# A weight block split earlier in the mask stage, one block moved ahead of it and one behind it: a hybrid decoder block on one Trainium2 core

## The chip, the core and the metric

The kernel runs on one core of one Trainium2 chip. A core has a matrix engine (TensorE, PE in the rows; PEld is its weight load), a vector engine (VectorE, DVE), a scalar engine (ScalarE, ACT), GpSimd (POOL) and SyncE (SP), which here issues nearly all DMAs. Each engine works through its own queue in order; semaphores tie the queues together. The metric is the device time of one execution in microseconds (us). TensorE's clock has two levels, 1.2 and 2.4 GHz; the profile gives the granted clock as a share of the higher one.

## The reference

```python
def reference(x, p, ...):                       # x: (1, 512, 1024) float32
    xn = _rmsnorm(h, ln_mix_g[i]); z = xn @ w_in[i]
    ...                                          # S5 scan, spatial gating, output projection
    h = h + mix @ w_out[i]
    hn = _rmsnorm(h, ln_ffn_g[i])
    h = h + _peer(hn, peer_wq[i], peer_keys[i], peer_u[i], peer_v[i])
    gate = jax.nn.sigmoid(_rmsnorm(h, ple_norm_g[i]) @ ple_w_gate[i])
    h = h + gate * (p[i] @ ple_w_proj[i])
    return _rmsnorm(h, final_g)

def _peer(xn, wq, keys, u_tab, v_tab):           # 16384 experts = 128 x 128 product keys
    q = (xt @ wq).reshape(t, 8, 2, 128)
    sc = einsum('thkd,hknd->thkn', q, keys)
    ...                                          # top 16 of each half, top 16 of the sums
    gates = softmax(top_s)
    act = gelu(einsum('td,thkd->thk', xb, u_tab[experts])) * gates
    return einsum('thk,thkd->td', act, v_tab[experts])
```

The change lies in `_peer`.

## The kernel before

The experts are not gathered for most tokens. For 384 of the 512 tokens the kernel multiplies all 16384 rows of `u_tab` and of `v_tab` and masks the result; the first 128 tokens (`NS`) gather their experts by indirect DMA. The 128 x 128 experts make 128 blocks (`NK`) of 128 experts. A **u block** is one such block of `u_tab` times the normalised tokens: `b_mm` issues 24 matmuls (8 slices of the depth, three products of float32r high and low parts, by `mm3`), and ScalarE's gelu leaves the result in a slot of `gab`, or, for the blocks in the list `FAR`, in a tile `far` that a DMA writes to DRAM (`fard`) and a later one reads back. A u block's weights go through three steps: `b_load` (SP fetches `ust`, three buffers), `b_split` (ScalarE casts `ust` to the high part `uh`, then another engine subtracts to give the low part `ul`, two buffers each), `b_mm`. `b_step(n)` does `b_load(n + 3)`, `b_split(n + 1)`, `b_mm(n)`. `b_split` gives the subtraction to GpSimd in four pieces, except for u blocks numbered from `PREM` to `NPRE`, where VectorE does it in one. `UORD` is the order in which u blocks are taken.

The part of `tile_hybrid_block` around the change runs in this order, and the order is written out by hand:

- **Retrieval**: scores, top-16 lists, and u blocks 0 to 33 between them (`ahead(upto)` takes u blocks until number `upto` - 1). Then `softmax_b` on VectorE, and `slots`, which transposes indices and gates on TensorE and turns them into `keyn` and `gpart`.
- **Mask stage**: `one_hots(0)`, `ahead(PRE + PREX + PREY)`, which is u block 34, and 96 steps of 4 tokens. For each pair of steps VectorE makes one `onehot` tile (`one_hots`, two instructions, `OB` = 2 buffers); for each step TensorE multiplies 12 small bf16 matmuls out of it into `pgm`, and ScalarE copies `pgm` to `stg`. Steps 2k and 2k + 1 read one-hot tile k, and tile k + 1 is put into the queue ahead of step 2k. Every eight steps a DMA writes `stg` to `gd` in DRAM. After every fourth step stands a `b_step`: u blocks 35 to 58, 24 of them.
- **Main loop**: for each of the 128 blocks `r`, the masks `gread` come back from `gd`, `a_gate` multiplies them into the block's `gab` slot, `a_split` and `v_split` make `ah`, `al`, `vh`, `vl`, and `y_mm(r)` multiplies 24 matmuls of 512 columns (`yp`). The remaining u blocks 59 to 127 are taken here. Before `r` = 0 stand `a_gate(0)`, `a_split(0)`, `v_split(0)`, `a_gate(1)`; `r` = 0 takes u block 59 ahead of `y_mm(0)`. The tiles `vh`, `vl` lie in memory that the retrieval and mask stages' tiles have used, `far` among them, so that their first writer waits for the last DMA out of that memory.

The lines that set the counts before:

```python
PRE = 33; PREX = 1; PREY = 1; NPRE = AHEAD + SPILL   # 59
PREM = PRE + PREX + PREY                             # 35
o = gw.tile([P, 4, TG // 2, NK, 2], BF16, name="onehot", bufs=OB)    # OB = 2
ahead(PRE + PREX + PREY + (n + 1) * (NPRE - PRE - PREX - PREY) // len(steps))
```

Of the kernel before, what the change touches and what calls it, by code (L numbers as in the profile page):

```python
# [29 lines left out]
H = 8  # L30
# [10 lines left out]
AHEAD = 40  # L41
# [26 lines left out]
PRE = 33  # L68
SPILL = 19
GPIECE = 256  # L70
FLEAD = 24
PREX = 1
PREY = 1


# [2 lines left out]
NPRE = AHEAD + SPILL  # L78
PREM = PRE + PREX + PREY
UORD = []  # L80
for _i in range(AHEAD):
    UORD.append(_i)
    if _i >= PRE0 - SPILL // 2 and len(UORD) - _i - 1 < SPILL and _i % 2 == 0:
        UORD.append(FAR[len(UORD) - _i - 1])
UORD += FAR[len(UORD) - AHEAD:]
UORD += [_b for _b in range(NK) if _b not in UORD]
assert sorted(UORD) == list(range(NK)) and set(UORD[:NPRE]) == set(range(AHEAD)) | set(FAR)

# [16 lines left out]
def tile_hybrid_block(ctx: ExitStack, tc: tile.TileContext, x, p_t, cols_d, rows_d, w_in, s5_b, s5_c, glu_w, ws_t,  # L105
# [35 lines left out]
    def pst(name, pool=None):  # L141
        return (pool or ps).tile([P, 512], F32, name=name, tag="ps")
# [13 lines left out]
    def split_sb(hi, lo, src, eng=None, piece=GPIECE):  # L156


        S.copy(hi, src)  # L159
        if eng is not G:  # L160
            V.tensor_tensor(lo, src, hi.bitcast(F32), op=ALU.subtract)  # L161
            return
        h, l, s = (a if len(a.shape) == 2 else a.rearrange("p a b -> p (a b)") for a in (hi.bitcast(F32), lo, src))
        for o in range(0, l.shape[1], piece):
            sl = slice(o, o + piece)
            G.tensor_tensor(l[:, sl], s[:, sl], h[:, sl], op=ALU.subtract)  # L166
# [692 lines left out]
    def b_load(n):  # L859
        if n < NB:  # L860
            BS[n] = ub.tile([P, ND, P], F32, name="ust", bufs=3)
            nc.sync.dma_start(BS[n], wq[n] if n < 2 * H else ut[UORD[n - 2 * H]])

    def b_split(n, eng=G):
        if n < NB:
            hi = ub.tile([P, ND, P], F32R, name="uh")
            lo = ub.tile([P, ND, P], F32R, name="ul")
            if PREM <= n - 2 * H < NPRE + 1:
                split_sb(hi, lo, BS[n], V)
            else:  # L870
                split_sb(hi, lo, BS[n], eng, GPIECE if n < 2 * H + NPRE else D)
            BS[n] = hi, lo

    def b_mm(n):
        if n >= NB:
            return
        hi, lo = BS.pop(n)
        p_ = pst("pq", ps2)
        t0 = 0 if n < 2 * H else NS
        for c in range(ND):  # L880
            mm3(p_[:, 0:T - t0], (hi[:, c, :], lo[:, c, :]), (hn[c][0][:, t0:T], hn[c][1][:, t0:T]), c == 0, c == ND - 1)
        if n < 2 * H:
            QT[n] = qw.tile([P, T], F32, name="qt")
            S.copy(QT[n], p_)
        else:
            n = UORD[n - 2 * H]
            if n in FAR:
                t = fr.tile([P, TD], F32, name="far")
                S.activation(t, p_[:, 0:TD], AF.Gelu)
                nc.sync.dma_start(fard[FAR.index(n)], t)  # L890
            else:
                ga[n] = slot(n)
                S.activation(ga[n], p_[:, 0:TD], AF.Gelu)  # L893
# [5 lines left out]
    def far_load(n):  # L899
        ga[n] = slot(n)  # L900
        nc.sync.dma_start(ga[n], fard[FAR.index(n)])

    def b_step(n):
        b_load(n + 3)
        b_split(n + 1)
        b_mm(n)

    keys = qw.tile([P, 2 * H, NK], F32, name="keys", bufs=1)
# [115 lines left out]
    done = 1  # L1024

    def ahead(upto):
        nonlocal done
        while done < upto:
            b_step(2 * H + done)
            done += 1  # L1030
# [5 lines left out]
    for i in order:  # L1036
        S.activation(gates[i], gates[i], AF.Exp)
    ahead(PRE + PREX)
    for i in order:
# [27 lines left out]
    def v_load(r):  # L1067
        st = vg.tile([P, D], F32, name="vst")
        nc.sync.dma_start(st, uv[r * P:(r + 1) * P, D:])
        VS[r] = st  # L1070

    def g_load(r, n=NDC):
        if r % RG == 0:
            gr = vg.tile([P, NDC, RG, TC], F32, name="gread")
            nc.sync.dma_start(gr[:, 0:n].rearrange("p c r t -> p c (r t)"), gd[:, r // RG, 0:n, :])
            GR[r // RG] = gr
# [4 lines left out]
    steps = [(i, c, t0) for i in range(NS // P, NT) for c in range(P // TC) for t0 in range(0, TC, 4)]  # L1081
    OH = {}

    def one_hots(n):

        i, c, t0 = steps[n * TG // 4]
        keyn, gpart = trs[i]
        g = (c * TC + t0) // TG
        o = gw.tile([P, 4, TG // 2, NK, 2], BF16, name="onehot", bufs=OB)
        flat = lambda a: a.rearrange("p z t r e -> p (z t) r e")  # L1090
        two, three = [P, TG, NK, 2], [P, 3 * TG // 2, NK, 2]
        pairs = lambda a: a[:, g].rearrange("p z (t e) -> p (z t) e", e=2)[:, :, None, :]
        V.tensor_tensor(o[:, 2:4], keyno[:, None].to_broadcast([P, 2, TG // 2, NK, 2]), pairs(keyn).to_broadcast(two),
                        op=ALU.is_equal)
        V.tensor_tensor(flat(o[:, 0:3]), o[:, 2:3].to_broadcast([P, 3, TG // 2, NK, 2]), pairs(gpart).to_broadcast(three),
                        op=ALU.mult)
        OH[n] = o

    one_hots(0)
    ahead(PRE + PREX + PREY)  # L1100
    for n, (i, c, t0) in enumerate(steps):
        gn, ga0 = n * 4 // TG, n * 4 % TG
        if ga0 == 0 and (gn + 1) * TG < 4 * len(steps):
            one_hots(gn + 1)
        if n == len(steps) - VPRE:
            v_load(0)
            v_load(1)
        if t0 == 0:
            stg = gw.tile([P, NK, TC], F32, name="stg")
        pg = pst("pgm")  # L1110
        o = OH[gn]
        for a in range(4):
            for z in range(3):
                t, e = divmod(ga0 + a, 2)
                PE.matmul(pg[:, a * P:(a + 1) * P], o[:, 3, t, :, e], o[:, z, t, :, e], start=z == 0, stop=z == 2)
        S.copy(stg[:, :, t0:t0 + 4].rearrange("p r t -> p t r"), pg.rearrange("p (t r) -> p t r", t=4))
        if n == len(steps) - 1:
            V.tensor_copy(GR[0][:, NDC - 1], stg[:, 0:RG, :])
        if t0 + 4 == TC:
            nc.sync.dma_start(gd[:, :, (i * P - NS) // TC + c, :], stg.rearrange("p (a r) t -> p a (r t)", r=RG))  # L1120
            if n == len(steps) - 1 - TC // 4:
                g_load(0, NDC - 1)
        ahead(PRE + PREX + PREY + (n + 1) * (NPRE - PRE - PREX - PREY) // len(steps))
    gs.close()
    ret.close()

# [12 lines left out]
    def v_split(r):  # L1139
        st = VS[r]  # L1140
        vh = vb.tile([P, D], F32R, name="vh")
        vl = vb.tile([P, D], F32R, name="vl")
        split_sb(vh, vl, st, V)
        VS[r] = vh, vl

    def a_gate(r):
        if r < NK:
            a3 = ga[r].rearrange("p (c t) -> p c t", c=NDC)
            V.tensor_tensor(a3, a3, GR[r // RG][:, :, r % RG, :], op=ALU.mult)  # L1149
# [110 lines left out]
    a_split(0)  # L1260
    v_split(0)
    a_gate(1)
    for r in range(NK):
        if r + 2 < NK:
            v_load(r + 2)
        if r + 4 < NK:
            g_load(r + 4)
        if r + FLEAD in FAR:
            far_load(r + FLEAD)
        s0 = nb  # L1270
        while nb < ns[r]:
            n = 2 * H + nb
            b_load(n + 3)
            if n + 3 >= NB:
                wg_load(n + 3 - NB)
            b_split(n + 1)
            nb += 1
        while kg < min(NK, ks[r] + 2):
            gather(kg)
            kg += 1  # L1280
        k0 = kd
        while kd < ks[r]:
            dot_step(kd)
            kd += 1
        for n in range(s0, nb):
            assert UORD[n] - NAHEAD < r
            b_mm(2 * H + n)
        if r + 1 < NK:
            a_gate(r + 2)
            a_split(r + 1)  # L1290
            v_split(r + 1)
        if kd > k0:
            act_step(k0, kd - k0)
        for k in range(k0, kd):
            y_step(k)
        j = r - (NK - SEND)
        if 1 <= j:
            wg_load(j + 2)
        if 0 <= j <= 4:
            wg_split(j, WGE[j])  # L1300
        elif j == 5:
            wg_split(5, "V")
            wg_split(6, "V")
        if j == 0:
            assert kd == NK
            V.tensor_tensor(hsb[:, 0, :], hsb[:, 0, :], y0, op=ALU.add)
            row_tile(None, "fin", hrow0)
        if j == TR:
            t_rows(0, 0, ps2)
            t_rows(0, 1, ps2)  # L1310
        if j == TR + 1:
            t_norm(0)
        if r == NK - SEND - 4:
            assert nb - NK + NAHEAD >= 0 and r + 1 >= NK - NAHEAD + -(-NT * D // TD)
            hsb = gab[:, 0:NT * D].rearrange("p (i d) -> p i d", i=NT)
            for i in range(NT):
                nc.sync.dma_start(hsb[:, i, :], hd[i])
        y_mm(r)
# [91 lines left out]
```

## Time and profile before

| | us |
|---|---|
| median of 3 runs (1580.32 to 1581.36) | 1580.43 |
| the profiled execution's own time | 1581.07 |
| its span in the trace | 1579.4 |
| mask stage, from the first one-hot (485.73) to the last mask step's end (680.03) | 194.3 |
| main loop, from the first matmul of `y_mm(0)` (693.1) to those of the last `y_mm` (1524.1) | 831 |

The profile lists busy time per engine, and per line and tile. A row of the timeline gives start and duration of an instruction, then engine, line, operation, output and inputs, and in brackets how long the engine had been idle before it and what ended that. Instructions overlap a little at their ends, so the time that one takes from its engine is read from one start to the next.

### The profile page before, as it was taken

The numbers are of one execution on the slowest core, as the hardware profiler recorded it, in microseconds if no ns is written. First come the engines' busy times: TensorE is split into PE (matmuls) and PEld (weight loads), VectorE is DVE, ScalarE is ACT, GpSimd is POOL, SyncE is SP. The second block draws the span as 40 slices with busy tenths as digits, with TensorE's granted clock in tenths as the row PEclk, the third lists the DMA queues.
The fourth block names the chain that finished last, engine by engine and source line by source line (L and its number), as shares of the span: only waits on it lengthen the run. The fifth ranks groups of instructions, "written<-read, shape, count | busy, mean of one in ns | idle before, by whom it ended". The sixth has DMA issues, their size and how long they took to land.

```text
span 1579.4 us, 22413 instructions
## 1 busy us (share of the span) xinstructions
PE 1506.2 (95%) x8195; PEld 1305.6 (83%) x8195; DVE 1354.7 (86%) x2512; ACT 661.9 (42%) x1121; POOL 603.3 (38%) x478
## 2 busy tenths in 40 slices
PE   8799989999997888889999999999999999999998
PEld 5456778899997888878888888888888888888886
DVE  9897645899998888859898999999899999989774
ACT  3655433333335666643333333333333333333354
POOL 2001214477880000015455555545455455555201
PEclk9999999999999999999999999999999999999999
DMA  6132033224343566788899998899899989999841
GB/s 254 41 100 68 27 117 123 81 94 139 136 142 116 179 222 194 236 276 310 309 331 343 336 336 321 327 336 341 316 350 337 344 317 346 331 329 330 301 165 67
DMA packets 129711, 369.90 MB, mean 234 GB/s; under 512 B 9024, under 2 KB 63040, under 8 KB 113088
## 3 DMA queue, kind: packets, MB, share of 16 engines
q1 hardware_dynamic: 111168, 234.24, 42.7%
q0 software_dynamic: 18432, 134.23, 22.9%
q8 instruction: 64, 1.05, 0.3%
q14 instruction: 47, 0.39, 0.1%
HBM read 333.24 MB, written 35.19 MB: 233 GB/s over the span
## 4 chain that ended last, share of the span: by engine, by line
PE 33%; issue 7%; DVE 6%; POOL 5%; DMA 5%; ACT 0%; POOLq 0%; DVEq 0%; ACTq 0%
PE yp L153 7%; PE yp L154 7%; PE yp L152 6%; DMA g<-in_uv,idx 5%; PE pq L154 3%; PE pq L152 3%; PE pq L153 3%; POOL ul L166 3%; POOL g L1135 2%; DVE vl L161 2%; DVE gab L1149 1%; DVE act L1171 1%; DVE g L1167 1%; PE pg L152 1%; PE pg L154 1%
## 5 line engine op out<-in xcount | busy, mean ns | idle before, releaser
L166 POOL TENSOR_TENSOR ul<-ust,uh 128x256 fp32r<-128x256 f32 (+1 forms) x268 | 359.6, 1367 | 369.5 <-ACT uh L159 369.3
L152 PE MATMUL pq<-hnh,uh 128*128 128x384 f32 (+1 forms) x1152 | 397.2, 345 | 0.8 <-DVE hnl L170 0.8
L154 PE MATMUL pq<-hnh,ul 128*128 128x384 f32 (+1 forms) x1152 | 394.7, 343 | 1.7 <-POOL ul L166 1.7
L153 PE MATMUL pq<-hnl,uh 128*128 128x384 f32 (+1 forms) x1152 | 393.4, 342 | 0.0
L1135 POOL DMA_INDIRECT g<-in_uv,idx x128 | 209.1, 1634 | 313.6 <-DVE y L1178 298.1
L153 PE MATMUL yp<-vl,ah 128*128 128x512 f32 x768 | 303.4, 395 | 10.1 <-DVE vl L161 10.0
L152 PE MATMUL yp<-vh,ah 128*128 128x512 f32 x768 | 300.8, 392 | 4.4 <-ACT vh L159 4.4
L154 PE MATMUL yp<-vh,al 128*128 128x512 f32 x768 | 302.0, 393 | 0.0
L893 ACT ACTIVATE gab<-pq 128x384 f32<-128x384 f32 x109 | 53.7, 492 | 429.5 <-PE pq L154 429.5
L154 PEld LDWEIGHTS pq<-hnh,ul 128*128 128x128 f32 x1152 | 216.6, 188 | 8.6 <-POOL ul L166 3.1
L152 PEld LDWEIGHTS pq<-hnh,uh 128*128 128x128 f32 x1152 | 216.9, 188 | 8.2 <-DVE hnl L170 1.0
L153 PEld LDWEIGHTS pq<-hnl,uh 128*128 128x128 f32 x1152 | 216.9, 188 | 7.4 <-DVE hnl L170 0.2
L161 DVE TENSOR_TENSOR vl<-vst,vh 128x1024 fp32r<-128x1024 f32 x128 | 164.5, 1285 | 25.0 <-ACT vh L159 24.6
L153 PEld LDWEIGHTS yp<-vl,ah 128*128 128x128 f32 x768 | 145.1, 189 | 44.6 <-DVE vl L161 15.9
L1167 DVE SCALAR_TENSOR_TENSOR g<-g,hrow 128x1024 f32<-128x1024 f32 x128 | 158.0, 1236 | 20.3 <-DMA g<-in_uv,idx 20.2
L152 PEld LDWEIGHTS yp<-vh,ah 128*128 128x128 f32 x768 | 145.3, 189 | 33.7 <-ACT vh L159 4.8
L154 PEld LDWEIGHTS yp<-vh,al 128*128 128x128 f32 x768 | 145.2, 189 | 30.1
L1178 DVE SCALAR_TENSOR_TENSOR y<-g,act,y 128x1024 f32<-128x1024 f32 x127 | 163.2, 1285 | 4.5
L159 ACT CAST uh<-ust 128x1024 fp32r<-128x1024 f32 x144 | 151.4, 1052 | 3.3 <-DMA ust<-in_wq 3.3
L1171 DVE TENSOR_TENSOR act<-act,gate 128x1 f32<-128x1 f32 (+1 forms) x117 | 145.4, 1243 | 0.0
L159 ACT CAST vh<-vst 128x1024 fp32r<-128x1024 f32 x128 | 134.2, 1048 | 12.0 <-issue 6.5
L159 ACT CAST ah<-gab 128x384 fp32r<-128x384 f32 x128 | 65.1, 509 | 105.2 <-issue 85.5
(418 smaller groups left out, 1912.3 us busy)
## 6 DMA issues: line engine op xcount, KB each, us to landing
ust<-in_ut SPq DMA_DIRECT2D x128, 512.0 KB, 6.8
vst<-in_uv SPq DMA_DIRECT2D x128, 512.0 KB, 6.5
gd<-stg SPq DMA_DIRECT2D x12, 2048.0 KB, 8.2
gread<-gd SPq DMA_DIRECT2D x31, 768.0 KB, 8.7
ust<-in_wq SPq DMA_DIRECT2D x16, 512.0 KB, 3.2
wstage<-in_w_in SPq DMA_DIRECT2D x12, 512.0 KB, 7.7
wstage<-in_w_out SPq DMA_DIRECT2D x8, 512.0 KB, 3.2
ust<-in_ple_wg SPq DMA_DIRECT2D x8, 512.0 KB, 5.2
```

What stands on the lines that cost most here:

```text
L152: PE.matmul(o, lh, rh, start=start, stop=False)
L153: PE.matmul(o, lh, rl, start=False, stop=False)
L154: PE.matmul(o, ll, rh, start=False, stop=stop)
L159: S.copy(hi, src)
L161: V.tensor_tensor(lo, src, hi.bitcast(F32), op=ALU.subtract)
L166: G.tensor_tensor(l[:, sl], s[:, sl], h[:, sl], op=ALU.subtract)
L893: S.activation(ga[n], p_[:, 0:TD], AF.Gelu)
L1135: G.indirect_dma_start(out=gt, out_offset=None, in_=uv, in_offset=bass.IndirectOffsetOnAxis(ap=idx[:, r:r + 1], axis=0))
L1149: V.tensor_tensor(a3, a3, GR[r // RG][:, :, r % RG, :], op=ALU.mult)
L1167: V.scalar_tensor_tensor(GS[k][:, 0:D], GS[k][:, 0:D], 1.0, hrow0, op0=ALU.mult, op1=ALU.mult, accum_out=dots[:, k:k + 1])
L1171: V.tensor_tensor(act[:, k:k + n], act[:, k:k + n], gates[0][:, k:k + n], op=ALU.mult)
L1178: V.scalar_tensor_tensor(y0, t[:, D:], act[:, k:k + 1], y0, op0=ALU.mult, op1=ALU.add)
```

## The change

`PREX` becomes 2, so `PREM` becomes 36: one u block more (34) is taken ahead of `softmax_b`, the block after `one_hots(0)` is now number 35, and 22 blocks (36 to 57) are spread over the 96 mask steps, one in every 4.36 steps. `b_prepare` takes load and split out of `b_step`; the mask loop calls it for a block one step ahead of the step after which that block stands, in front of that earlier step's one-hot and matmuls. The last of the first 59 u blocks, number 58, is taken by a new `ahead(NPRE)` after `a_gate(1)`. `UORD` moves block 39 to the end of the first 59, so that number 58 has its slot in `gab` and number 57 is the last one of `FAR`.

```diff
-PREX = 1
+PREX = 2
...
 UORD += FAR[len(UORD) - AHEAD:]
+UORD.append(UORD.pop(UORD.index(AHEAD - 1)))
 UORD += [_b for _b in range(NK) if _b not in UORD]
...
+    prepared = set()
+
+    def b_prepare(n):
+
+        if n not in prepared:
+            prepared.add(n)
+            b_load(n + 3)
+            b_split(n + 1)
+
     def b_step(n):
-        b_load(n + 3)
-        b_split(n + 1)
+        b_prepare(n)
         b_mm(n)
...
     one_hots(0)
-    ahead(PRE + PREX + PREY)
+    ahead(PREM)
+    due = lambda n: PREM + (n + 1) * (NPRE - 1 - PREM) // len(steps)
     for n, (i, c, t0) in enumerate(steps):
+        if n + 1 < len(steps) and due(n + 1) > max(due(n), done):
+            b_prepare(2 * H + done)
...
-        ahead(PRE + PREX + PREY + (n + 1) * (NPRE - PRE - PREX - PREY) // len(steps))
+        ahead(due(n))
...
     a_gate(1)
+    ahead(NPRE)
     for r in range(NK):
```

Where the blocks and splits stand now is shown on three queues. First ScalarE early in the mask stage; `COPY stg` is the copy behind one mask step, `CAST uh` opens a split, and `ACTIVATE gab` is the gelu behind a u block. Before:

```order
L1116 COPY stg_5046<-pgm_5047 128x4x128
L1116 COPY stg_5046<-pgm_5061 128x4x128
L1116 COPY stg_5046<-pgm_5078 128x4x128
L1116 COPY stg_5046<-pgm_5092 128x4x128
L159 CAST uh_5108<-ust_4914 128x1024
L893 ACTIVATE gab_1867<-pq_5112 128x384
```

The same place of the change, steps 3 to 8:

```order
L1128 COPY stg_4891<-pgm_4943 128x4x128
L1128 COPY stg_4891<-pgm_4960 128x4x128
L894 ACTIVATE gab_1867<-pq_4974 128x384
L1128 COPY stg_4891<-pgm_5000 128x4x128
L1128 COPY stg_4891<-pgm_5017 128x4x128
L160 CAST uh_5033<-ust_4854 128x1024
L1128 COPY stg_4891<-pgm_5037 128x4x128
L1128 COPY stg_5055<-pgm_5056 128x4x128
L894 ACTIVATE gab_1867<-pq_5070 128x384
```

The cast has moved ahead of two copies, and the u block's gelu stands behind four copies before, and here behind step 4 and again behind step 8, with step 5's copy after it.

On TensorE in the change, the last matmul of step 4 and the head of the u block that follows it (`pq` is a u block's output):

```order
L1127 MATMUL pgm_4960<-onehot_4920 128x128
L153 MATMUL pq_4974<-hnh0_1920,uh_4856 128x384
L154 MATMUL pq_4974<-hnl0_1921,uh_4856 128x384
L155 MATMUL pq_4974<-hnh0_1920,ul_4857 128x384
L153 MATMUL pq_4974<-hnh0_1920,uh_4856 128x384
```

Step 5, behind the block's 24 matmuls, reads the same tile, `onehot_4920`; before, a block stands only between two steps that read different tiles.

Last, ScalarE at the end of the mask stage (`far` is the gelu of a block of `FAR`, `ah` and `vh` are the main loop's first casts). Before:

```order
L1116 COPY stg_6968<-pgm_7093 128x4x128
L1116 COPY stg_6968<-pgm_7107 128x4x128
L159 CAST uh_7125<-ust_6931 128x1024
L889 ACTIVATE far_7154<-pq_7129 128x384
L159 CAST ah_7179<-gab_1867 128x384
L159 CAST vh_7183<-vst_6768 128x1024
L159 CAST uh_7194<-ust_7028 128x1024
L893 ACTIVATE gab_1867<-pq_7202 128x384
```

And now:

```order
L1128 COPY stg_6939<-pgm_7070 128x4x128
L1128 COPY stg_6939<-pgm_7084 128x4x128
L890 ACTIVATE far_7125<-pq_7100 128x384
L160 CAST ah_7150<-gab_1867 128x384
L160 CAST vh_7154<-vst_6739 128x1024
L160 CAST uh_7161<-ust_6968 128x1024
L894 ACTIVATE gab_1867<-pq_7165 128x384
L160 CAST uh_7197<-ust_7064 128x1024
L894 ACTIVATE gab_1867<-pq_7205 128x384
```

The cast of u block 59, `uh_7125` before and `uh_7161` now, has moved from ahead of `vh` to behind it, and a second gelu has come between.

## Rows read from the trace of the kernel before

**Rows 1.** The page: busy time, share of the span and instructions of each engine.
```profile
PE 1506.2 (95%) x8195; PEld 1305.6 (83%) x8195; DVE 1354.7 (86%) x2512; ACT 661.9 (42%) x1121; POOL 603.3 (38%) x478
```
**Rows 2.** Stretches: us, then busy us of PE, PEld, DVE, ACT, POOL, clock, DMA, GB/s.
```profile
487.00:684.00 197.00, 172.47 (x1730) 164.57 (x1729) 168.78 (x122) 129.50 (x144) 0.00 (x0) 1.00 0.62 201
...
1000.00:1100.00 100.00, 97.27 (x471) 85.33 (x470) 92.61 (x113) 36.30 (x64) 51.03 (x26) 1.00 0.90 330
```

**Rows 3.** Waits from 486 to 680 us, by engine: us in total, times, longest.
```profile
DVE ul L161 <- ACT uh L159: 23.0, 23, 1.0
...
PE pgm L1115 <- DVE onehot L1095: 24.5, 25, 2.5
```

**Rows 4.** Timeline of one cycle of four mask steps, most matmuls left out.
```profile
500.93 1.55 PE L1115 MATMUL pgm<-onehot 128*128 128x128 bf16 x24 [0.90 <-DVE onehot L1095]
...
502.29 0.42 PE L152 MATMUL pq<-hnh,uh 128*128 128x384 f32 x1
...
503.70 1.09 ACT L159 CAST uh<-ust 128x1024 fp32r<-128x1024 f32 x1
...
504.82 1.23 DVE L161 TENSOR_TENSOR ul<-ust,uh 128x1024 fp32r<-128x1024 f32 x1 [1.02 <-ACT uh L159]
...
505.96 1.22 DVE L1093 TENSOR_TENSOR onehot<-keyno,keyn 128x2048 bf16<-128x2048 bf16 x1
...
506.54 1.56 PE L1115 MATMUL pgm<-onehot 128*128 128x128 bf16 x24
...
507.22 1.76 DVE L1095 TENSOR_TENSOR onehot<-onehot,gpart 128x3072 bf16<-128x3072 bf16 x1
...
508.89 1.22 DVE L1093 TENSOR_TENSOR onehot<-keyno,keyn 128x2048 bf16<-128x2048 bf16 x1
...
509.03 1.55 PE L1115 MATMUL pgm<-onehot 128*128 128x128 bf16 x24 [0.93 <-DVE onehot L1095]
```

**Rows 5.** Timeline between retrieval and masks: POOL, PE and DVE.
```profile
475.30 3.45 POOL L166 TENSOR_TENSOR ul<-ust,uh 128x256 fp32r<-128x256 f32 x4 [3.57 <-ACT uh L159]
...
479.80 0.45 PE L1046 MATMUL trp<-ident,gate 128*128 128x128 f32 x1 [3.89 <-DVE gate L995]
...
481.42 0.67 PE L152 MATMUL pq<-hnh,uh 128*128 128x384 f32 x1
...
485.73 1.22 DVE L1093 TENSOR_TENSOR onehot<-keyno,keyn 128x2048 bf16<-128x2048 bf16 x1
```

**Rows 6.** Timeline: VectorE operations without POOL at work (the first) and beside it.
```profile
468.55 0.23 DVE L967 SCALAR_TENSOR_TENSOR ia<-pos,ia 128x64 f32<-128x64 f32 x1
...
469.04 0.69 DVE L969 SCALAR_TENSOR_TENSOR t<-ia,t 128x64 f32<-128x64 f32 x1
...
699.45 2.48 POOL L166 TENSOR_TENSOR ul<-ust,uh 128x1024 fp32r<-128x1024 f32 x1 [0.17 <-ACT uh L159]
...
699.59 2.75 DVE L1149 TENSOR_TENSOR gab<-gab,gread 128x384 f32<-128x384 f32 x1
```

**Rows 7.** Timeline from the last mask step into the main loop: PE, SP and ACT.
```profile
680.03 0.42 PE L152 MATMUL pq<-hnh,uh 128*128 128x384 f32 x1
...
682.27 4.86 SPq L862 DMA_DIRECT2D ust<-in_ut  x1
...
684.55 0.49 ACT L889 ACTIVATE far<-pq 128x384 f32<-128x384 f32 x1 [2.07 <-issue]
...
687.18 0.45 SPq L890 DMA_DIRECT2D fard<-far  x1
...
691.98 1.04 ACT L159 CAST vh<-vst 128x1024 fp32r<-128x1024 f32 x1 [6.54 <-issue]
...
693.07 0.80 PE L152 MATMUL yp<-vh,ah 128*128 128x512 f32 x1 [4.45 <-ACT vh L159]
...
699.62 0.49 PE L153 MATMUL yp<-vl,ah 128*128 128x512 f32 x1
...
700.87 0.33 PE L152 MATMUL pq<-hnh,uh 128*128 128x384 f32 x1
```

## The prediction

> **What bounds the kernel now.** I read the busy shares first, then the stretches, then the waits of the one stage that the diff touches, then its timeline. TensorE is busy for 95% of the span [rows 1] and in the main loop for 97 of 100 us [rows 2]: whatever delays the start of the main loop is paid in full at the end. The mask stage is another matter: 172.5 of 197 us on TensorE and 168.8 on VectorE [rows 2], and each waits for another engine. VectorE waits 23 times, 1.0 us each, for ScalarE's cast `uh` [rows 3]; TensorE's 24.5 us of waiting are for one-hots, so VectorE's chain sets the pace. One cycle shows it [rows 4], from one start to the next: two one-hot instructions take 1.26 and 1.67 us of VectorE, 2.93 a tile; the subtraction `ul` takes 1.14; two mask steps take 1.36 of TensorE, 0.68 each; a u block takes 4.25. The cast starts only when the copies of two mask steps are out of ScalarE's way: from the first of these matmuls (500.93) to the subtraction (504.82) are 3.89 us, of which VectorE stands idle for 1.02. The cycle is 8.10 us.
>
> **The mask stage, by VectorE's chain.** The stretch is from the first subtraction's end to the last one-hot's end: 47 tiles on either side.
>
> *Fewer splits.* 23 subtractions lie in it before, 21 after (those of blocks 37 to 57; that of 58 comes behind the last one-hot): 2 x 1.14 = -2.3 us.
>
> *The old wait.* 23.0 us go [rows 3], if nothing takes their place. Two things do.
>
> *Blocks between two steps of one tile.* At one block in 4.36 steps, the 22 blocks stand after steps 4, 8, 13, 17, 21, 26, 30, 34 and so on: 10 after an even step and 12 after an odd one. An even step 2k and its partner 2k + 1 read the same one-hot tile, and TensorE now has the block between them. There are two buffers, so tile k + 2 can't be written until step 2k + 1 is done. Let tile k be ready at zero. TensorE: 0.05 to start, 0.68 for step 2k, 4.25 for the block, 0.85 for step 2k + 1 with the end of its last matmul, 0.05 back: 5.9 us. VectorE meanwhile has one subtraction and tile k + 1: 1.14 + 2.93 = 4.07 us, less the 0.08 by which it is free before its result counts. It waits 1.85 us. No row of before shows this wait, since there a block never stood there; it is built from rows alone, and its bounds are 1.5 (if VectorE comes there late from the wait below) and 2.0. 10 x 1.85 = +18.5.
>
> *Blocks between two tiles.* The cast has moved ahead of two copies, and the subtraction ahead of one tile; so the cast still stands behind the second copy of the pair that VectorE finished one tile earlier, as before. The wait stays. It is 1.0 where TensorE takes that pair at once; where the preceding block stands in front of the pair, it is longer: with a tile ready at zero and the wait x ahead of it, the block ends at 5.7, the pair's subtraction can start at 5.7 + 3.89 = 9.6, and VectorE is there at x + 1.14 + 2 x 2.93 = x + 7.0. With x = 0.95 that is a wait of 1.6; with x = 1.6, 1.0. Worked on so, a run of three gives 0.95, 1.7 and 1.1. The same working gives 1.1 for the cycle of before, where the rows have 1.0, so I take 0.1 off: 1.15 on average, bounds 0.9 and 1.6. Eleven of the twelve lie ahead of the last one-hot: +12.6.
>
> Sum of the stage: -2.3 - 23.0 + 18.5 + 12.6 = **+5.8 us**, bounds +1 and +11. ScalarE's copies, casts and gelus (129.5 of 197 us busy [rows 2]) and the loads that now stand ahead of `gd` writes on SP aren't late for anyone: a load is issued two blocks, some 17 us, ahead of its cast.
>
> **Between retrieval and masks.** Block 34 fills TensorE's 3.89 us of waiting for gates [rows 5], which costs nothing and gains nothing by itself: VectorE sets when the first one-hot starts (485.73). What comes with it is block 35's subtraction, taken from VectorE (where block 36's takes its place) to GpSimd: four more pieces, right behind the four that end at 478.75. They run beside `softmax_b`. What that does, VectorE's small operations show: 0.23 us without GpSimd at work, 0.69 beside it, and one with two inputs lasted 2.75 beside a piece of 2.48 [rows 6]. Four pieces took 3.45 us in all [rows 5]. VectorE's operations slip in between pieces, and some of the softmax's may not be held at all, so I take a little under half: **+1.5 us**, bounds 0 and 3.4. The Trainium skill (SBUF — State Buffer, "SBUF: two separate sides") calls this an exclusive lock on a shared pair of ports, taken by a GpSimd operation, a VectorE operation with two SBUF inputs or one in a 2-port mode, for the whole instruction. The 2.75 beside 2.48 agrees with it; by the lock alone the delay would be close to the upper bound and the total 1.9 us higher.
>
> TensorE then waits some 3.4 us for the first one-hot: block 35 starts about 1.2 us later than its forerunner did (481.42) and takes 4.25, to 486.9; the tile is ready at 485.73 + 1.5 + 2.93 + 0.1 = 490.3. The clock was lost after the idle 3.89 us (the block after it ran at half speed, 1.2 GHz) and not in the mask stage after 2.5 [rows 2, 3, 5]; 3.4 lies between. If it is lost, block 36 runs at half speed and holds tile 4 for up to 4 us. I leave it out of the sum and keep it for the range.
>
> **Into the main loop.** Call T the start of the u block behind the last mask step, 680.03 before [rows 7]. Before: blocks 58 and 59 run until T + 8.5; `vh` starts at T + 11.95, which the row puts down to "issue". In the program this cast carries the waits of the last two `far` writes, whose memory it reuses; the write was issued at 687.18, behind a weights load that held SP for 4.86 us. `y_mm(0)` starts at T + 13.04, its first 15 matmuls at half speed until 699.62, and ends at T + 20.84. After: the last `FAR` block is 57, still the one behind the last mask step, so `vh` still waits for its write; but no weights load stands ahead of it on SP. Its gelu ends at T + 5.0; I take the cast at T + 10.5, bounds 8.5 and 12. Blocks 57 and 58 last until T + 8.5, as 58 and 59 did. Block 59 is the new thing: its cast now stands behind `vh` in ScalarE's queue and its subtraction behind `vl` and a gate on VectorE. Cast 11.5 to 12.5; subtraction, behind `vl` (1.14) and the gate (0.55), 13.3 to 14.5. The third matmul of block 59 needs it: T + 14.5, after 6 us with two matmuls in them, so at half speed as before, until about 19. Then 7.6 of its matmuls are left at 0.173: 20.4, and `y_mm(0)` at full speed, 5.5 us: T + 25.9. Against 20.84 that is **+5.0 us**, bounds +2 and +8 (the far write; GpSimd's split of block 60 getting ahead of the subtraction). Both kernels have the same u blocks behind them there, 0 to 59. The block meant for the gap doesn't shorten it, since the gap's end hasn't moved and one block more stands behind it.
>
> **Sum.** 5.8 + 1.5 + 5.0 = 12.3 us. On the profiled execution's 1581.07 that is 1593.4; the median of the runs is 0.64 lower, so **1592.7**, 0.8% slower.
>
> **The rivals.** (a) *The early split does what it says* (faster). If VectorE never finds a buffer taken and each cast is ready, the stage loses 25.3 us instead of gaining 5.8: 1592.7 - 31.1 = 1561.6. For it: TensorE would then have 96 x 0.68 + 22 x 4.25 = 159 us of work and VectorE 162, either of them less than the stage now takes. Against it: two buffers, and the block standing between a tile's two steps. It decides at tile k + 2 behind such a block: whether it starts as tile k + 1 ends, or 1.8 us later. Chance 0.10. (b) *`vh` no longer waits for the far write*: then cast and subtraction of block 59 are done by T + 9 and TensorE goes on without a gap: `y_mm(0)` ends near T + 18.8, 2.0 less than now, not 5.0 more: 1585.7. For it: block 39, without a far write, comes last. Against: the block ahead of it has one. Chance 0.12. (c) *The waits change hands one for one*: the stage +0 to -2 (each mid-tile wait 1.2), the head hidden, the gap filled in part: near 1581. Chance 0.08. (d) *The clock is lost at the head* and GpSimd's pieces cost their full 3.4: 1592.7 + 4 + 1.9 = 1598.6. Chance 0.10.
>
> **How the numbers follow.** The forecast, 1587 to 1597, has 0.60. Range 1583 to 1599: the forecast, (b) and (d), 0.82; it leaves out (a) and most of (c). A measurement of this kernel can tell about 0.2%, 3.2 us, from no change. Slower: 0.60 + 0.12 + 0.10 = 0.82; within 0.2%: (c), 0.08; faster: (a), 0.10. The base is the runs' median, and the three runs lie within 1.1 us, which the range swallows.
>
> **What would show it.** The mask stage's waits should list `onehot` waiting for the mask matmuls about 10 times, 1.8 us each, where before it had none, and `ul` waiting for `uh` some 12 times. The last mask step should end some 7 us later than 680.03. Behind it, TensorE should run two u blocks, wait for `uh` and `ul` of block 59, then run that block and only then `y_mm(0)`. The head should show GpSimd at work until about 482 and the first one-hot near 487. I am wrong if the one-hots don't wait, or if the main loop, whose TensorE has 2.7 us idle in 100 [rows 2], takes up some of the delay.

## The result and the profile after

The changed kernel takes 1591.01 us (median of 5 runs, 1588.96 to 1592.35) where the kernel before takes 1581.24 beside it (5 runs, 1580.32 to 1583.97). The ratio is 1.0058, with a 95% interval from 1.0043 to 1.0072: it is slower by 9.2 us (the medians differ by 9.8), and the prediction was 1592.7. The profiled execution took 1591.53 us, with a span of 1589.8.

The busy line of the page shows about the same work as before. Of the two stretches, the mask stage has TensorE busy for 163.66 of 200 us, where before it was 172.47 of 197; a hundred us of the main loop are as before (columns as in [rows 1, 2]):

```profile
PE 1508.9 (95%) x8195; PEld 1307.4 (82%) x8195; DVE 1354.3 (85%) x2511; ACT 661.7 (42%) x1121; POOL 607.8 (38%) x482
```
```profile
489.00:689.00 200.00, 163.66 (x1667) 155.38 (x1668) 166.28 (x119) 126.38 (x139) 0.00 (x0) 0.99 0.61 193
1000.00:1100.00 100.00, 98.16 (x478) 86.51 (x477) 91.30 (x111) 35.84 (x64) 50.97 (x26) 1.00 0.92 336
```

The mask stage has two u blocks less and still is longer: 199.46 us from the first one-hot (487.62) to the last mask step's end (687.08), against 194.30. VectorE's waits in it up to the last one-hot (us in total, times, longest) stand where [rows 3] has one line of 23.0:

```profile
DVE onehot L1102 <- PE pgm L1127: 18.0, 10, 1.8
DVE ul L162 <- ACT uh L160: 8.9, 9, 1.7
DVE ul L162 <- PE pgm L1127: 3.3, 2, 1.6
```

The first line is a wait that the kernel before doesn't have. The timeline of the first block that stands between two steps of one tile, with most of its matmuls left out, shows how it comes about:

```profile
497.68 0.85 PE L1127 MATMUL pgm<-onehot 128*128 128x128 bf16 x12 [1.39 <-DVE onehot L1104]
498.34 0.42 PE L153 MATMUL pq<-hnh,uh 128*128 128x384 f32 x1
498.74 1.22 DVE L1102 TENSOR_TENSOR onehot<-keyno,keyn 128x2048 bf16<-128x2048 bf16 x1
499.99 1.76 DVE L1104 TENSOR_TENSOR onehot<-onehot,gpart 128x3072 bf16<-128x3072 bf16 x1
...
502.59 2.25 PE L1127 MATMUL pgm<-onehot 128*128 128x128 bf16 x36
...
503.50 1.22 DVE L1102 TENSOR_TENSOR onehot<-keyno,keyn 128x2048 bf16<-128x2048 bf16 x1 [1.75 <-PE pgm L1127]
```

Step 4 takes its 12 matmuls at 497.68, the block runs from 498.34 to 502.59, and only then comes step 5, which reads the same tile. VectorE has finished the other buffer by 501.75 and can't begin the next tile before step 5 is through, at 503.50: 1.75 us of idle time. The 36 matmuls in the 502.59 row are steps 5 to 7.

Behind the last mask step (T' = 687.08), where [rows 7] has the place before:

```profile
687.08 0.42 PE L153 MATMUL pq<-hnh,uh 128*128 128x384 f32 x1
...
691.59 0.49 ACT L890 ACTIVATE far<-pq 128x384 f32<-128x384 f32 x1 [2.88 <-issue]
...
692.11 2.11 SPq L891 DMA_DIRECT2D fard<-far  x1
...
697.39 1.04 ACT L160 CAST vh<-vst 128x1024 fp32r<-128x1024 f32 x1 [4.91 <-DMA fard<-far]
...
699.43 0.69 PE L153 MATMUL pq<-hnh,uh 128*128 128x384 f32 x1 [3.76 <-ACT uh L160]
...
701.35 0.69 PE L155 MATMUL pq<-hnh,ul 128*128 128x384 f32 x1 [0.91 <-DVE ul L162]
...
706.93 0.39 PE L153 MATMUL yp<-vh,ah 128*128 128x512 f32 x1
...
711.05 0.33 PE L153 MATMUL pq<-hnh,uh 128*128 128x384 f32 x1
```

`vh` waits for the last `far` write, block 59's cast stands behind it, and TensorE idles for 3.76 and 0.91 us ahead of block 59. The landing times of the DMAs point to what the `far` write itself waits for. The last mask write, 2048 KB, is issued just ahead of it, at 688.74, and lands 8.0 us later, at 696.7; the `far` write, 192 KB, lands 0.6 us behind it, at 697.3. Before, the mask write landed at 689.9 (681.65 + 8.2), then the weights load of 512 KB that stood ahead of the `far` write, at 691.4, then the `far` write, at 691.9.

`y_mm(0)` ends at T' + 23.97, against T + 20.84 before. Stage and tail together are 5.16 + 3.13 = 8.3 us longer, and the runs say 9.2. The two profiled spans differ by 10.4: 1.9 of it is there by the first one-hot, and 1.8 of that by 81 us, ahead of all changed code. It is not in every profile (the first one-hot of the experiments' kernels below starts anywhere from 485.74 to 490.06).

### The profile page after: what moved, and what is told of

Same layout as the page of the kernel before. It is cut to its first block, busy times and chain, and to the rows that moved or that the text cites. A ratio compares the mean times of both kernels' runs of the same rounds, so it can differ in the third digit from the quotient of the medians.

```text
span 1589.8 us, 22413 instructions
## 1 busy us (share of the span) xinstructions
PE 1508.9 (95%) x8195; PEld 1307.4 (82%) x8195; DVE 1354.3 (85%) x2511; ACT 661.7 (42%) x1121; POOL 607.8 (38%) x482
## 4 chain that ended last, share of the span: by engine, by line
PE 54%; DVE 26%; issue 8%; POOL 6%; DMA 4%; ACT 2%; POOLq 0%; DVEq 0%; ACTq 0%
PE yp L154 7%; PE yp L155 7%; PE yp L153 7%; PE pq L153 6%; PE pq L155 6%; PE pq L154 6%; DMA g<-in_uv,idx 3%; POOL ul L167 3%; DVE onehot L1104 3%; POOL g L1147 3%; PE pz L593 3%; DVE onehot L1102 2%; PE pgm L1127 2%; DVE vl L162 1%; DVE oh L989 1%
## 5 line engine op out<-in xcount | busy, mean ns | idle before, releaser
L167 POOL TENSOR_TENSOR ul<-ust,uh 128x256 fp32r<-128x256 f32 (+1 forms) x272 | 363.3, 1360 | 372.7 <-ACT uh L160 362.5
L153 PEld LDWEIGHTS pq<-hnh,uh 128*128 128x128 f32 x1152 | 217.1, 188 | 12.3 <-ACT uh L160 4.1
L1127 PE MATMUL pgm<-onehot 128*128 128x128 bf16 x1152 | 75.7, 221 | 37.7 <-DVE onehot L1104 37.7
```

Source lines behind the costliest of these rows:

```text
L153: PE.matmul(o, lh, rh, start=start, stop=False)
```

## The experiments

Nine kernels were run. The first four shared the runs of before (1581.86 us), the next four did too (1580.60), the last had its own (1580.77). The table has, for each profile, the mask stage (first one-hot to the last mask step's end), the tail (from there to the end of `y_mm(0)`), what both differ from before's 194.30 and 20.84, and what the timed runs differ from before, which is (ratio - 1) times the runs of before:

| kernel | stage, us | tail, us | sum against before | measured against before (95%) | ratio (95%) |
|---|---|---|---|---|---|
| after | 199.46 | 23.97 | +8.3 | +9.2 (6.8 to 11.4) | 1.0058 (1.0043 to 1.0072) |
| e2_odd | 192.80 | 25.65 | +3.3 | +3.3 (0.9 to 5.9) | 1.0021 (1.0006 to 1.0037) |
| e5_spacing | 199.12 | 26.24 | +10.2 | +10.1 (6.6 to 13.6) | 1.0064 (1.0042 to 1.0086) |
| e3_sooner | 198.68 | 17.71 | +1.3 | +0.6 (-1.6 to 2.8) | 1.0004 (0.9990 to 1.0018) |
| e4_head | 194.31 | 14.90 | -5.9 | -6.0 (-8.5 to -3.6) | 0.9962 (0.9946 to 0.9977) |
| e6_split59 | 200.55 | 16.76 | +2.2 | +3.8 (1.4 to 6.3) | 1.0024 (1.0009 to 1.0040) |
| e7_farlast | 194.21 | 12.53 | -8.4 | -7.1 (-9.6 to -4.6) | 0.9955 (0.9939 to 0.9971) |
| e8_cast | 173.43 | 24.53 | -17.2 | -15.8 (-21.7 to -9.8) | 0.9900 (0.9863 to 0.9938) |
| e9_cast_head | 173.45 | 22.86 | -18.8 | -17.4 (-21.5 to -13.1) | 0.9890 (0.9864 to 0.9917) |
| e10_cast_far | 173.45 | 13.08 | -28.6 | -26.4 (-30.2 to -22.4) | 0.9833 (0.9809 to 0.9858) |

In each row the sum of the two stretches lies within the interval of the timed runs. Each profile is of a single execution, and outside the two stretches the profiles differ too: the rest of the main loop, from the end of `y_mm(0)` to the last `y_mm`, takes 823.5 us before and from 819.6 (e6) to 827.5 (e3; 827.2 in e7) in the others. In seven of the ten kernels, what the profile gains or loses outside the two stretches is, to 0.5 us, what the profiled execution lies off the median of its kernel, so it looks like variation between executions. In the changed kernel, e7 and e10, 1.6 to 2.6 us stay unexplained.

**e2_odd: the changed kernel, with blocks behind odd steps only.** It takes the placement of the 22 blocks apart from the rest.

```diff
-    due = lambda n: PREM + (n + 1) * (NPRE - 1 - PREM) // len(steps)
+    due = lambda n: PREM + (n + 1) // 2 * 2 * (NPRE - 1 - PREM) // len(steps)
```

> The changed kernel, with its 22 blocks moved by at most one step, so that each stands behind an odd mask step, that is between two one-hot tiles; the early split stays. Theory (a block between two steps of one tile holds the tile's buffer): the waits of one-hots for mask matmuls, 10 of 18.0 us in all in the changed kernel, are gone; the waits of the subtraction for the cast grow from some 12 to some 25 us, 1.2 each; the mask stage, 199.5 us from the first one-hot to the last mask step's end, falls to about 193, and the time by 6 us, to some 1585. Rival (the early split itself makes the stage longer, wherever the block stands): the stage stays at 199 or more.

VectorE's waits in its mask stage:

```profile
DVE ul L162 <- ACT uh L160: 22.0, 19, 1.5
DVE ul L162 <- PE pgm L1127: 1.9, 2, 0.9
```

The 18.0 us of one-hots waiting for mask matmuls are gone to the last one: a block between a tile's two steps is what makes them. The stage is 6.7 us shorter than the changed kernel's, not 18: the waits for the cast have gone from 8.9 + 3.3 = 12.2 us to 23.9. So a split one step sooner leaves VectorE waiting for it as long as before the change.

**e5_spacing: the changed kernel without the early split in the mask loop.**

```diff
     for n, (i, c, t0) in enumerate(steps):
-        if n + 1 < len(steps) and due(n + 1) > max(due(n), done):
-            b_prepare(2 * H + done)
         gn, ga0 = n * 4 // TG, n * 4 % TG
```

> The changed kernel without the early split in the mask loop: load and split stand right ahead of each block again, the 22 blocks at every 4.36 steps. Theory (the wait behind a block in mid-tile comes from the spacing alone): 10 waits of one-hots for mask matmuls, some 18 us, remain; the mask stage is 196 to 199 us, the time within 3 us of the changed kernel. Rival (the early split makes these waits): they go, and the stage falls to 185 or less, the time to some 1577.

```profile
DVE onehot L1102 <- PE pgm L1125: 17.3, 10, 2.1
DVE ul L162 <- ACT uh L160: 11.5, 12, 1.0
```

Stage and waits are those of the changed kernel: its early split neither gains nor costs anything there. In the tail it gains 2.3 us (23.97 against 26.24 here): without it the weights load stands ahead of the last `far` write again, and `vh` starts at T + 11.6 instead of T' + 10.3.

**e3_sooner: the kernel before, with the early split alone** (blocks after every fourth step, as before).

```diff
     def b_step(n):
-        b_load(n + 3)
-        b_split(n + 1)
+        b_prepare(n)
         b_mm(n)
...
+    due = lambda n: PREM + (n + 1) * (NPRE - PREM) // len(steps)
     for n, (i, c, t0) in enumerate(steps):
+        if n + 1 < len(steps) and due(n + 1) > max(due(n), done):
+            b_prepare(2 * H + done)
...
-        ahead(PRE + PREX + PREY + (n + 1) * (NPRE - PRE - PREX - PREY) // len(steps))
+        ahead(due(n))
```

> The kernel before, with only load and split taken one step sooner in the mask stage (blocks where they were, behind every fourth step). Theory (the cast still stands behind the copies of the pair of steps that follows the last block): VectorE's wait for the cast stays, 22 or 23 times, 1.0 to 1.4 us each; the mask stage is 194 to 200 us, so 1581 to 1587. Rival (the cast is ready in time once it is issued a step sooner): the 23 us of waiting go, the stage falls to about 171 and the time to about 1558.

```profile
DVE ul L161 <- ACT uh L159: 23.6, 18, 2.5
DVE ul L161 <- PE pgm L1125: 4.7, 5, 1.0
```

No block stands inside a tile here, no one-hot waits, and the subtraction still waits 28.3 us, 5.3 more than in [rows 3]. The stage is 4.4 us longer. The time is the same, since the tail is 3.1 shorter: the weights load that stood ahead of the last `far` write on SP has been issued sooner, the write goes out at T + 5.0 instead of T + 7.2, and `vh` starts at T + 9.9 instead of T + 11.95.

**e4_head: the kernel before, with block 39 last and that block at the head of the main loop.**

```diff
+UORD.append(UORD.pop(UORD.index(AHEAD - 1)))
...
-        ahead(PRE + PREX + PREY + (n + 1) * (NPRE - PRE - PREX - PREY) // len(steps))
+        ahead(min(NPRE - 1, PREM + (n + 1) * (NPRE - PREM) // len(steps)))
...
     a_gate(1)
+    ahead(NPRE)
     for r in range(NK):
```

> The kernel before, with only the end changed: block 39 last of the first 59, and that block multiplied at the main loop's head instead of behind the last mask step (blocks 35 to 57 stay behind every fourth step). Theory (the gap ahead of the main loop is the wait of the first vh cast for the last far write): that write is now one block older, vh no longer waits for it, block 59's split comes in time, and from the last mask step's end to the end of y_mm(0) are about 16 us instead of 20.84: about 1576. Rival (a block at the head costs, since block 59's split stands behind vh): about 24 us as in the changed kernel, 1584.

This part of the change is a gain of 6.0 us where the mask loop's spacing is left alone. The cast `vh` here:

```profile
683.04 1.04 ACT L160 CAST vh<-vst 128x1024 fp32r<-128x1024 f32 x1
```

It starts at T + 2.9 with no wait, because the last block of `FAR` now stands after step 91, four steps earlier, so that its write is issued ahead of the last mask write, and no block stands after step 95. The same lines in the changed kernel have the last `far` block behind the last step, since its 22 blocks are spread over all 96.

**e6_split59: the changed kernel, with block 59's split ahead of `vh`.**

```diff
     nb = NPRE
+    b_prepare(2 * H + done)
     a_gate(0)
```

> The changed kernel with one line more: the split of u block 59 is issued ahead of the first gate and of vh, so that its cast comes before vh in ScalarE's queue and its subtraction before vl on VectorE. Theory (the changed kernel's tail is long because block 59's split stands behind vh): block 59's matmuls follow block 58's without a gap, TensorE's only idle stretch ahead of y_mm(0) is gone or under 1.5 us, y_mm(0) ends at T + 18.3 where the changed kernel has T + 23.97; about 5.7 us sooner than the changed kernel, near 1586 where before is 1581.5. Rival (the late far write alone holds the tail): vh still arrives at T + 10.5 and y_mm(0) still ends near T + 24; the time stays within 2 us of the changed kernel's 1591.

```profile
698.39 1.05 ACT L160 CAST vh<-vst 128x1024 fp32r<-128x1024 f32 x1 [2.20 <-DMA fard<-far]
```

`vh` still starts at T + 10.4, but block 59's cast is through by then: TensorE has no gap, and the tail is 7.2 us shorter than the changed kernel's. So the gap came from block 59's split, queued behind `vh`; the late far write by itself is hidden by the extra block.

**e7_farlast: the kernel before, with two blocks that go to `gab` last.**

```diff
+for _b in (AHEAD - 2, AHEAD - 1):
+    UORD.append(UORD.pop(UORD.index(_b)))
```

> The kernel before with two u blocks that go to gab moved to the end of the first 59, so that the last block that goes by a far tile is 56 instead of 58 and its write is some 16 us older when the mask stage ends; nothing else is moved. Theory (vh waits for the last far write, which stands behind a weights load on SP): vh starts near T + 5.5 instead of T + 11.95, y_mm(0) starts at about T + 8.5 without the idle 4.45 us and ends near T + 14 instead of T + 20.84: 6.8 us sooner, near 1574.7 where before is 1581.5. Rival (vh waits for something else that is late, such as the last write of the masks or the copies): vh stays near T + 11.9, y_mm(0) ends near T + 21, and the time is within 2 us of before.

```profile
685.19 1.05 ACT L161 CAST vh<-vst 128x1024 fp32r<-128x1024 f32 x1
...
688.36 0.39 PE L154 MATMUL yp<-vh,ah 128*128 128x512 f32 x1
```

`vh` starts at T + 5.2 and `y_mm(0)` at T + 8.4 without idle time and at full speed (0.39 us a matmul, where [rows 7] has 0.80). The 6.54 us that [rows 7] put down to "issue" were the wait for the far write: only the order of the last blocks was changed. The last far write is now issued at 675.38, ahead of the last mask write (681.57), and not at 687.18, behind it.

**e8_cast: the kernel before, with only the cast moved, two copies ahead.** The subtraction and the block stay.

```diff
+    def b_cast(n):
+        if n < NB and n not in CAST:
+            hi = ub.tile([P, ND, P], F32R, name="uh")
+            lo = ub.tile([P, ND, P], F32R, name="ul")
+            S.copy(hi, BS[n])
+            CAST[n] = hi, lo
...
+        if n in CAST:
+            hi, lo = CAST.pop(n)
+            V.tensor_tensor(lo, BS[n], hi.bitcast(F32), op=ALU.subtract)
+            BS[n] = hi, lo
...
     for n, (i, c, t0) in enumerate(steps):
+        if n % 4 == 2:
+            b_cast(2 * H + done + 1)
```

> The kernel before with only the cast uh moved: it is issued ahead of the copies of the last two mask steps in front of a u block, on its own; the subtraction and the block stay where they are. Theory (VectorE's chain paces the mask stage, and the 23 us of ul waiting for uh come from the cast's place behind two copies; no block comes between two steps of one tile): the 23.0 us go and nothing takes their place, since VectorE's own work, 47 tiles of 2.93 and 24 subtractions of 1.14, is 165 us and TensorE's 96 x 0.68 + 24 x 4.25 = 167 us: the stage takes about 173 us instead of 194.3, and the time is near 1560 where before is 1581.5. Rival (the waits change hands: with two one-hot buffers VectorE must wait for the mask matmuls or TensorE for the one-hots all the same): onehot waiting for the mask matmuls appears with 10 us or more, the stage takes 190 us or more, and the time is 1577 or above.

VectorE's only wait in its mask stage:

```profile
DVE onehot L1106 <- PE pgm L1130: 2.9, 11, 0.3
```

The 23.0 us are gone, 2.9 take their place, and the stage is 20.9 us shorter. The tail grew by 3.7, which the forecast had not seen:

```profile
664.18 1.05 ACT L870 CAST uh<-ust 128x1024 fp32r<-128x1024 f32 x1 [2.60 <-DMA ust<-in_ut]
665.13 1.94 ACT L1131 COPY stg<-pgm 128x512 f32<-128x512 f32 x2
```

The last early cast reaches the head of ScalarE's queue before its weights have landed, and the last two mask copies, now behind it, wait with it. The last mask write and the last far write behind it come some 4 us later (T + 5.7 and T + 11.2 instead of T + 1.6 and T + 7.2), and with them `vh`.

**e9_cast_head: e8 and e4 together.** Its edits are those two.

> The kernel before with the cast of e8 and the block at the head of e4 (block 39 last of the first 59 and taken behind the second gate) together. Theory (the two gains lie in different stretches, and the main loop doesn't take them back): the stage near 173 us and y_mm(0)'s end near T + 15, that is 21 + 6 = 27 us sooner than before, near 1554.5 where before is 1581.5. Rival (the main loop's work behind is late anyway, for instance by weights that come from DRAM or by the masks that are read back): a part of the 27 us comes back as idle time of TensorE in the main loop, which gets longer than 824 us, and the time is 1560 or above.

The stage is e8's, but the tail is 22.86 us instead of 15, and the stated rival, a longer main loop, is not why (820.3 us behind `y_mm(0)`, before 823.5). TensorE's gap there and VectorE's subtraction ahead of it:

```profile
668.72 2.47 POOL L167 TENSOR_TENSOR ul<-ust,uh 128x1024 fp32r<-128x1024 f32 x1 [189.87 <-ACT uh L160]
668.91 3.36 DVE L877 TENSOR_TENSOR ul<-ust,uh 128x1024 fp32r<-128x1024 f32 x1
...
672.33 0.69 PE L155 MATMUL pq<-hnh,ul 128*128 128x384 f32 x1 [8.25 <-DVE ul L877]
```

Here too the last early cast waits 2.58 us for its weights and holds up the copies; block 59's subtraction then stands behind the gates and `vl`, and falls beside a GpSimd subtraction, where it lasts 3.36 us instead of 1.22. This is read from the trace; no run takes it apart.

**e10_cast_far: e8's cast, but not for the last block, and e7's order.**

```diff
+for _b in (AHEAD - 2, AHEAD - 1):
+    UORD.append(UORD.pop(UORD.index(_b)))
...
+        if n % 4 == 2 and n < len(steps) - 2:
+            b_cast(2 * H + done + 1)
```

> The kernel before with the early cast of e8 (not for the last block, whose weights arrived late in e8 and held up the mask copies) and with the two gab blocks at the end of the first 59 as in e7. Theory (the two gains lie in different stretches and add up; e7's main loop gave back 3.7 us of 8.3): the mask stage near 173.4 us against 194.3, y_mm(0)'s end near T + 12.5 to 15 against 20.84, the main loop up to 4 us longer: 23 to 28 us sooner than before, 1553 to 1558 where before is 1581. Rival (what is saved ahead of the main loop comes back in it, since its weights and masks are then late): TensorE idles in the main loop, which gets longer than 830 us, and the time is no better than e8's 1563.

It takes 1555.07 us (6 runs, 1552.74 to 1559.42) against 1580.77, ratio 0.9833 (0.9809 to 0.9858), and beats both kernels. Both gains are kept: the tail is e7's but for 0.6 us, so leaving out the early cast of the last block took away what e8's tail had lost. The main loop behind `y_mm(0)` takes 823.7 us, as before (823.5). In its mask stage TensorE and VectorE are now both nearly always at work, 164 and 165 of 170 us where [rows 2] has 172 and 169 of 197:

```profile
487.00:657.00 170.00, 164.12 (x1662) 158.39 (x1661) 165.26 (x120) 124.57 (x140) 0.00 (x0) 1.00 0.68 220
```

One of its cycles, beside [rows 4]: the cast at 502.93 stands ahead of two copies, so it is out before VectorE gets to the subtraction at 504.74, which follows the one-hot without idle time.

```profile
502.93 1.06 ACT L872 CAST uh<-ust 128x1024 fp32r<-128x1024 f32 x1
...
503.06 1.76 DVE L1110 TENSOR_TENSOR onehot<-onehot,gpart 128x3072 bf16<-128x3072 bf16 x1
...
503.89 2.13 ACT L1133 COPY stg<-pgm 128x512 f32<-128x512 f32 x2
504.74 1.22 DVE L878 TENSOR_TENSOR ul<-ust,uh 128x1024 fp32r<-128x1024 f32 x1
```

A third one-hot buffer, which might let a block stand inside a tile without the wait, wasn't tried, and whether there is room for it isn't shown.

## Why the prediction was right, step by step

**The mask stage, +5.8 predicted, +5.2 measured.** Each term has its line. The waits of a block inside a tile: 10 x 1.85 = 18.5 predicted, 18.0 in 10 measured, and e2 shows that they belong to the even steps. The waits that stay between two tiles: 12.6 in 11 predicted, 8.9 + 3.3 = 12.2 in 11 measured. (The 3.3 are the same wait, put down to the mask matmuls whose copies stand ahead of the cast.) The old 23.0 go, and two splits fewer take off 2.3; the terms as measured give 18.0 + 12.2 - 23.0 - 2.3 = 4.9. Rival (a) fell on the point that was named for it: tile k + 2 starts 1.75 us late. And e8 shows how much rival (a) was worth, 20.9 us, had the cast alone been moved. In the change cast and subtraction moved together: each stands one step sooner in its own queue, so the one waits for the other as before.

**Between retrieval and masks, +1.5 predicted, 0 measured.** This term was mis-sized. From the start of GpSimd's pieces to the first one-hot are 487.62 - 477.13 = 10.49 us, and before 485.73 - 475.30 = 10.43 [rows 5]. The pieces are there, eight in a row, and the softmax's operations beside them are as long as before:

```profile
477.13 6.52 POOL L167 TENSOR_TENSOR ul<-ust,uh 128x256 fp32r<-128x256 f32 x8 [3.57 <-ACT uh L160]
...
480.70 0.27 DVE L1002 TENSOR_REDUCE zs<-gate 128x8 f32<-128x128 f32 x1
481.01 0.20 DVE L1003 RECIPROCAL zs<-zs 128x8 f32<-128x8 f32 x1
481.25 0.29 DVE L1004 TENSOR_TENSOR gate<-gate,zs 128x128 f32<-128x128 f32 x1
...
487.62 1.22 DVE L1102 TENSOR_TENSOR onehot<-keyno,keyn 128x2048 bf16<-128x2048 bf16 x1
...
490.69 2.72 PE L1127 MATMUL pgm<-onehot 128*128 128x128 bf16 x24 [3.08 <-DVE onehot L1104]
```

The prediction took its price from operations that met GpSimd's pieces squarely (in [rows 6], the one of 0.69 us started 0.12 us into a piece of 0.74). It allowed for operations that slip in between pieces; in fact all four of the softmax's two-input operations did. Taken one by one, the last four pieces start at 480.60, 481.34, 482.10 and 482.85 and last about 0.8 us each, and the four gate multiplies start at 481.25, 482.01, 482.77 and 483.53, each some 0.12 us before a piece ends. Reduce and reciprocal, which have one input, were as long as before in the middle of the pieces. The other kernels with eight pieces, e2, e5 and e6, have the same timing and the same 10.5 us; no run shifts it, so that the head is free because of it is argued, not shown.

The rule of the Trainium skill that the prediction weighed (SBUF — State Buffer, "SBUF: two separate sides") gives the shared pair of ports to whichever starts first, a GpSimd operation or a VectorE operation with two SBUF inputs, for the whole instruction. These multiplies neither show nor refute it; a subtraction that started 0.19 us behind a GpSimd piece of 2.47 us, in e9, agrees with it (3.36 us instead of 1.22).

One sign came true by luck: the first one-hot stands at 487.62, near the 487 that was named, but 1.8 of the 1.9 us were there by 81 us.

The clock was lost, as the range allowed: after the idle 3.08 us the first 24 mask matmuls took 2.72 us, and the granted clock was 0.50 from 491 to 493, 0.83 from 493 to 494 and 1.00 from 494 to 497. It cost nothing that shows, as the next tile was only ready at 494.7. Rival (d) priced it at 4 us on the assumption that the low clock lasts through block 36; it had returned before.

**Into the main loop, +5.0 predicted, +3.1 measured.** The mechanism holds at every point: `vh` at T' + 10.3 (10.5 predicted), behind the far write, which the row names; block 59's third matmul at T' + 14.3 (14.5); e6 and e7 show the two causes one by one. Two sizes were off. `y_mm(0)` has 18 matmuls, not 24 as said ahead of the prediction (the trace has three sorts of 768, over 128 blocks): at 0.23 us each 4.1 us instead of 5.5, which is 1.4 of the 1.9 too much. The rest is the clock, which returned at T' + 17.9 and not at 19. Rival (b) fell: the last far block is still behind the last mask step, and `vh` waits for it.

**The sum.** 12.3 predicted, 8.3 by the two stretches, 9.2 by the runs. The two errors, 1.5 and 1.9, have the same sign, and with 0.6 of the mask stage they make up the 4.0. The median, 1591.0, lies 1.7 us below the forecast and not 4.0: the runs of before beside it lie 0.8 above the earlier ones, and the medians differ by 1.5 more than the two stretches. These 2.3 us of closeness are luck.

## What to carry to other kernels

When one engine waits for another's result, move the producer alone; moving producer and consumer together by the same step moves the wait along with them (e3, e5: no gain; e8: 21 us). Before a piece of work is put between two others, ask which buffer the later one still holds and who waits for that buffer: here a u block of 4.25 us between two steps of one tile cost 1.75 us each time, with two buffers. And where a stage's memory is reused by the next, look for the youngest DMA out of it, and for a large one ahead of it in the queue: ordering the blocks so that the last far write went out 11.8 us sooner, ahead of the 2048 KB mask write, was worth 7.1 us for two lines (e7).

## What the hardware showed that was not expected

A wait that the trace puts down to "issue" can be a DMA's: the first `vh` had [6.54 <-issue] before, [4.91 <-DMA fard<-far] in the changed kernel, and none in e7, where the last far write is older.

The first DMA that SP issues right behind the last mask write of 2048 KB is held in its issue, whichever DMA it is, until 5.4 to 5.8 us after that write was issued. For a weights load this is 4.79 to 5.20 us of SP (e4 and e10; 4.86 in [rows 7]), against 0.38 and 0.63 for the two loads ahead of that write in e10. In the changed kernel the far write itself is held, for 2.11 us. It is issued at T' + 5.0, not T + 7.2, and still lands only behind the mask write.

TensorE's granted clock fell to 0.50 in an idle stretch of 3.08 us at the mask stage's head and was back within 3.3 us of the engine's resuming (0.83 from 493 to 494; the matmuls of 494.75 took 1.54 us for 24). It fell too ahead of block 59, in 3.76 us of idle time, and was back about 5.5 us after the engine had resumed.
